# A new instruction clock for the planner, and weight halves merged, in a two-layer hybrid block on one Trainium2 core

## The chip, the cores and the metric

The kernel runs on one core of one Trainium2 chip. The metric is the device time of one execution in microseconds (us), read as the median of several runs. The engines are named as in the profile: PE is the tensor engine (PEld its weight loads), DVE the vector engine, ACT the scalar engine, POOL the GpSimd engine, SP the sync engine, whose queue issues nearly all DMAs.

## What is computed

The reference is two layers of a hybrid block over 256 tokens with 2048 features, all in 32-bit floats:

```python
for l in range(DEPTH):                                  # DEPTH = 2
    h = rms_norm(x, attn_norm_g[l])
    proj = h @ w_in[l]                                  # 2048 -> 3664
    y_ssd = ssd_mixer(proj[..., :c0], proj[..., c0:c1], proj[..., c1:c2], ...)
    y_mla = mla_mixer(proj[..., c2:c3], proj[..., c3:c4], proj[..., c4:], ...)
    mixed = jnp.concatenate([y_ssd, y_mla], axis=-1) @ w_out[l]
    x = x + mixed
    x = x + memory_cross_attention(rms_norm(x, ...), rms_norm(mem, ...), ...)
    x = x + swiglu(rms_norm(x, ffn_norm_g[l]), w_gate[l], w_up[l], w_down[l])   # hidden 5632
```

`ssd_mixer` is a causal convolution over four tokens with SiLU, a state-space scan over two chunks of 128 tokens, a gate and a normalization. `mla_mixer` is causal attention of eight heads from two latents of 512 features.

## The kernel before

**Products in three parts.** Every large product takes 32-bit weights and activations apart into a rounded part (`hi`, the tensors ending in `h`) and the rest (`lo`, ending in `l`), and adds three products: x-high times w-high, x-high times w-low, x-low times w-high. A *chunk* is 512 rows of a weight by 512 columns (368 or 384 in some products). Its four row blocks of 128, two token tiles and three parts make 24 products on PE (`mm_chunk`, line 509), each 128x128 by 512 columns.

**Weights.** `load_w` (line 488) loads a chunk by one DMA into `raw` (three buffers). Before the change the chunk is then handled in two halves of two row blocks each: `hi` is a rounding copy of half of `raw`, made by `copy` on ACT or DVE, whichever the planner finds free first (ACT in nearly all cases), and `lo` is `raw` minus `hi`, made on DVE. Each has six buffers of half a chunk. The very first chunk is loaded and handled in four pieces.

**Order.** No engine's order is that of the program text. A `Recorder` collects all instructions, and `issue()` (line 269) runs a rough clock over them: at each step it gives every engine the instruction of its own that can start first by the clock (ties by program order, with `hi` and `lo` of weights 400 places ahead of theirs), takes the earliest of all, and advances that engine's clock by `cost()` (line 243). Results are ready a fixed `LAG` of 0.35 us after the end; a transposing DMA counts 2.2 us on its queue and 1.6 us more until it has landed. The chosen order is then fixed: on the chip each engine and each queue runs its list in that order, and an instruction whose data isn't there holds up all that stand behind it on its engine.

**Stages of a layer.** First the latent projections, then three `conv_part`s (line 775; the third makes `bcT`, the B and C of the scan, which PE then transposes or multiplies), `ssd_prep` (line 942), two gate products `z_part`, four `ssd_core`s (line 1014), `ssd_finish` (line 1043), and four `mla_proj` / `mla_attn` pairs (lines 819 and 885). `out_proj` (line 1094) begins with the scan's part of its input (`ysT`) and goes on with the attention's part (`ymT`). Cross-attention and the feed-forward part follow. In `ssd_prep`, POOL makes `xd`, `xw` and `y` by seven instructions over 512 or 1024 elements a partition, next to the time at which DVE makes `bcT` by twelve multiply-adds.

Of the kernel before, what the change touches and what calls it, by code (L numbers as in the profile page):

```python
# [8 lines left out]
F32 = mybir.dt.float32  # L9
# [7 lines left out]
P = 128  # L17
# [22 lines left out]
# the vectors of a layer that have a value per feature: column and number of blocks of 128 features  # L40
# [12 lines left out]
class View:  # L53
    """a view of a tile that is allocated only when its first instruction is issued."""
# [84 lines left out]
class Slot:  # L139
    """a tile of a pool; slots of a pool's tag are given out by the scheduler."""  # L140
# [47 lines left out]
class Recorder:  # L188
    """Instructions in program order; issue() gives them to Tile in an order in which, by a rough
    clock, each engine always takes the first of its instructions that has its data."""  # L190
# [13 lines left out]
    def add(self, *ways):  # L204
        """one instruction; `ways` are the (engine, method, function, arguments) that it may be issued as."""
# [37 lines left out]
    def cost(self, engine, method, args, kw, writes, reads):  # L243
# [7 lines left out]
        if engine == "PE":  # L251
            n = args[0].free_size()
            if method == "transpose":
                return 0.1075, self.LAG
            passes = 1 if args[1].tile.dtype == F32R else 4
            return max(passes * n / 2400 + 0.003, 0.107), self.LAG
        ptr = sum(0.07 for v in reads if v.free_size() == 1)
        if engine == "ACT":
            return 0.09 + n * 0.833e-3 + ptr, self.LAG
# [7 lines left out]
        return 0.065 + n * (0.52e-3 if fast else 1.04e-3) + ptr, self.LAG  # L267

    def issue(self, margin):
# [18 lines left out]
        def slot_time(op):  # L288
            """when the slots that op's new tiles need are free; None when they are not to be given yet"""
# [18 lines left out]
        while left:  # L308
# [30 lines left out]
            at[e] = start + cost  # L339
            op.end = at[e] + lag  # L340
# [31 lines left out]
def hybrid_kernel(ctx: ExitStack, tc: tile.TileContext, const, vec, rows, x_in, x_tr, mem, mem_tr, positions, w_in, w_q_b,  # L372
# [6 lines left out]
    def copy(out, src, scale=None, engines=(A, V)):  # L379
        """out = src * scale, on whichever of the engines is free first."""  # L380
# [30 lines left out]
    def nm(s):  # L411
        uid[0] += 1
        return f"{s}_{uid[0]}"
# [4 lines left out]
    def chunk_T(name):  # L418
        """a chunk of 512 features, transposed: the part of 12 significant bits and the rest."""
        return b4([P, 4, S], name + "h", F32R), b4([P, 4, S], name + "l", F32R)  # L420
# [21 lines left out]
    # zero-padded rotary queries of the two heads of a pair  # L442
# [6 lines left out]
    # until the first weights are there, products that nothing reads start the tensor engine's full clock  # L449
# [26 lines left out]
    def rsqrt(v, shape, tag):  # L476
        """1/sqrt(v) for positive v."""
# [10 lines left out]
    def load_w(w, r0, c0, n, pieces=1):  # L488
        """512 rows and n columns of w: the parts of 12 significant bits and the rests, two row blocks a tile."""
        parts = []  # L490
# [6 lines left out]
        for half in range(2):  # L497
            hi = wpool.tile([P, 2, n], F32R, tag="hi", name=nm("hi"), bufs=6)
            lo = wpool.tile([P, 2, n], F32R, tag="lo", name=nm("lo"), bufs=6)
            for i in range(0, 2, 4 // max(pieces, 2)):  # L500
                k = slice(i, i + 4 // max(pieces, 2))
                rk = raw[:, 2 * half + k.start:2 * half + k.stop, :]
                copy(hi[:, k, :], rk)
                V.tensor_sub(lo[:, k, :], rk, hi[:, k, :].bitcast(F32))
            parts.append((hi, lo))
        rec.bias += 400
        return parts

    def mm_chunk(accs, xc, parts, n, first, last, tokens_outer=False):
        """accs[t] += x chunk (512 features, transposed, two parts) @ w chunk."""  # L510
        order = [(k, t) for k in range(4) for t in range(NT)]
        for k, t in sorted(order, key=lambda kt: kt[1]) if tokens_outer else order:
            hi, lo = parts[k // 2]
# [792 lines left out]
```

## Time and profile before

| | before |
|---|---|
| median of 3 runs | 2313.14 us (2311.99 to 2314.82) |
| span of the profiled execution | 2308.3 us |
| PE busy | 2288.8 us (99%) |
| DVE busy | 1458.9 us (63%) |
| ACT busy | 1242.4 us (54%) |
| POOL busy | 106.0 us (5%) |
| DMA, mean rate over the span | 203 GB/s |

The span runs from the first to the last instruction; the measured time lies 4.8 us above it. A product's record overlaps the next one, since the engine is pipelined; the distance from one start to the next tells what a product costs, and that is how PE's rows are read below. A wait is shown in brackets: the idle time before the instruction and what ended it.

### The profile page before, as it was taken

How to read it: one execution, taken by the hardware profiler on the slowest of the kernel's cores; microseconds unless marked ns; L12 is line 12 of the kernel's file. 1: busy time of each engine (PE TensorE's matmuls, PEld its weight loads, DVE VectorE, ACT ScalarE, POOL GpSimd, SP SyncE). 2: the span in 40 equal slices, each digit the busy share in tenths (PEclk: the TensorE clock that was granted, in tenths of full speed). 3: DMA queues.
4: the chain of work that ended last, by engine and by line, in shares of the span. 5: the costliest groups of instructions: out<-in, count | busy, mean ns of one | idle time of the engine just before them, and what ended most of it. 6: DMA issues, size and time to landing. Idle time of an engine off the chain costs nothing.

```text
span 2308.3 us, 27311 instructions
## 1 busy us (share of the span) xinstructions
PE 2288.8 (99%) x10454; PEld 1911.4 (83%) x10454; DVE 1458.9 (63%) x2068; ACT 1242.4 (54%) x1839; POOL 106.0 (5%) x92
## 2 busy tenths in 40 slices
PE   9999999999999999999999999999999999999999
PEld 8878888888888888888898688888888888888887
DVE  7888876755545555455768887767555455554554
ACT  7767666644434444344566586666444344444442
POOL 0030200000000000000000311000000000000000
PEclk9999999999999999999999999999999999999999
DMA  9856687666656666566777566766676566665664
GB/s 311 244 161 182 183 259 215 183 198 209 210 188 200 208 201 208 186 208 199 212 221 223 150 186 191 227 199 185 199 212 208 186 208 200 201 210 184 207 208 139
DMA packets 361269, 467.91 MB, mean 203 GB/s; under 512 B 142385, under 2 KB 165553, under 8 KB 361137
## 3 DMA queue, kind: packets, MB, share of 16 engines
q1 hardware_dynamic: 361104, 466.16, 65.9%
q8 instruction: 82, 1.34, 0.3%
q14 instruction: 51, 0.41, 0.1%
q0 software_dynamic: 32, 0.00, 0.0%
HBM read 429.94 MB, written 2.10 MB: 187 GB/s over the span
## 4 chain that ended last, share of the span: by engine, by line
PE 93%; DVE 4%; DMA 1%; ACT 1%; issue 1%; SPq 0%; POOL 0%; ACTq 0%
PE acc L368 89%; PE tp L368 4%; DVE lo L368 2%; DMA ht<-hs 1%; DVE bcT L368 1%; ACT hi L368 0%; DMA raw<-in_w_in_dram 0%; DVE ysTl L368 0%; DVE whole L368 0%; DVE hs L368 0%; DVE kv L368 0%; DVE dec L368 0%; SPq L368 0%; POOL qkr L368 0%; ACT xTh L368 0%
## 5 line engine op out<-in xcount | busy, mean ns | idle before, releaser
L368 DVE TENSOR_TENSOR lo<-raw,hi 128x1024 fp32r<-128x1024 f32 (+3 forms) x818 | 984.8, 1205 | 764.4 <-ACT hi L368 762.2
L368 ACT CAST hi<-raw 128x1024 fp32r<-128x1024 f32 (+3 forms) x817 | 842.1, 1032 | 933.6 <-PE acc L368 870.9
L368 PE MATMUL acc<-hi,xTh 128*128 128x512 f32 (+1 forms) x1984 | 762.5, 384 | 1.3 <-ACT hi L368 1.3
L368 PE MATMUL acc<-lo,xTh 128*128 128x512 f32 (+1 forms) x1984 | 762.5, 384 | 1.1 <-DVE lo L368 0.9
L368 PE MATMUL acc<-hi,xTl 128*128 128x512 f32 (+1 forms) x1984 | 763.0, 385 | 0.0
L368 PEld LDWEIGHTS acc<-hi,xTh 128*128 128x128 f32 x1984 | 372.9, 188 | 72.8 <-ACT hi L368 2.6
L368 PEld LDWEIGHTS acc<-lo,xTh 128*128 128x128 f32 x1984 | 373.2, 188 | 72.2 <-DVE lo L368 1.9
L368 PEld LDWEIGHTS acc<-hi,xTl 128*128 128x128 f32 x1984 | 373.2, 188 | 71.0 <-issue 1.3
L368 PE MATMUL acc<-hi,hTh 128*128 128x512 f32 x704 | 273.5, 389 | 0.0
L368 PE MATMUL acc<-lo,hTh 128*128 128x512 f32 x704 | 273.5, 389 | 0.0
L368 PE MATMUL acc<-hi,hTl 128*128 128x512 f32 x704 | 273.5, 389 | 0.0
L368 PEld LDWEIGHTS acc<-lo,hTh 128*128 128x128 f32 x704 | 132.2, 188 | 27.5
L368 PEld LDWEIGHTS acc<-hi,hTl 128*128 128x128 f32 x704 | 132.1, 188 | 27.4
L368 PEld LDWEIGHTS acc<-hi,hTh 128*128 128x128 f32 x704 | 132.2, 188 | 27.4
L368 DVE TENSOR_TENSOR x<-x,acc 128x512 f32<-128x512 f32 x80 | 51.5, 681 | 13.3 <-PE acc L368 13.3
L368 POOL TENSOR_TENSOR rx_y<-rx_v,mhalf 128x2 f32<-128x2 f32 x6 | 8.1, 1352 | 1039.5 <-DVE rx_v L368 1004.7
L368 PE MATMUL acc<-lo,ysTh 128*128 128x512 f32 x128 | 51.4, 401 | 0.0
L368 PE MATMUL acc<-hi,ysTh 128*128 128x512 f32 x128 | 51.1, 399 | 0.0
L368 PE MATMUL acc<-hi,mTh 128*128 128x512 f32 x128 | 51.1, 399 | 0.0
L368 PE MATMUL acc<-lo,mTh 128*128 128x512 f32 x128 | 50.5, 395 | 0.0
L368 PE MATMUL acc<-hi,ysTl 128*128 128x512 f32 x128 | 50.5, 395 | 0.0
L368 PE MATMUL acc<-lo,ymTh 128*128 128x512 f32 x128 | 50.2, 393 | 0.0
(274 smaller groups left out, 1999.5 us busy)
## 6 DMA issues: line engine op xcount, KB each, us to landing
raw<-in_w_gate_dram SPq DMA_DIRECT2D x88, 1024.0 KB, 5.2
raw<-in_w_up_dram SPq DMA_DIRECT2D x88, 1024.0 KB, 5.3
raw<-in_w_down_dram SPq DMA_DIRECT2D x88, 1024.0 KB, 5.0
raw<-in_w_in_dram SPq DMA_DIRECT2D x40, 1024.0 KB, 5.5
raw<-in_w_out_dram SPq DMA_DIRECT2D x32, 1024.0 KB, 5.6
raw<-in_w_in_dram SPq DMA_DIRECT2D x23, 736.0 KB, 5.2
raw<-in_w_kv_b_dram SPq DMA_DIRECT2D x8, 1024.0 KB, 5.1
raw<-in_w_xk_dram SPq DMA_DIRECT2D x8, 1024.0 KB, 5.4
```

The source lines that it names most:

```text
L368: fn(*args, **kw)
```

## The change

Three things are edited: the price list `cost()`, one rule in `issue()`, and the granularity of `load_w` (with `mm_chunk`, which reads it).

- Prices in `cost()`: a rounded product of n columns goes from n / 2400 + 0.003 us to (n + 32) / 2400 us, a transpose on PE from 0.1075 to 0.067 us, a 32-bit product from four passes to two passes of twice the columns; the fixed part of an instruction on ACT goes from 0.09 to 0.2 us, with 0.19 us more for one that also writes a sum, and on DVE from 0.065 to 0.135 us. `LAG`, the DMA prices and POOL's prices stay.
- Rule in `issue()`: once a POOL instruction of more than 0.5 us (powers excepted) is given out, DVE's clock is moved to that instruction's end, if it isn't there yet.
- `load_w`: one `hi` and one `lo` instruction for a whole chunk of four row blocks. Buffers go from six halves to three wholes, the same bytes. The first chunk stays in four pieces.

Comments and docstrings are removed as well; nothing else of the kernel's text is touched. The core of the diff:

```diff
@@ cost
         if engine == "PE":
             n = args[0].free_size()
-            if method == "transpose":
-                return 0.1075, self.LAG
-            passes = 1 if args[1].tile.dtype == F32R else 4
-            return max(passes * n / 2400 + 0.003, 0.107), self.LAG
-        ptr = sum(0.07 for v in reads if v.free_size() == 1)
+            if method == "transpose" or args[1].tile.dtype == F32R:
+                return max(n + 32, 160) / 2400, self.LAG
+            return 2 * max((2 * n + 32) / 2400, 0.1), self.LAG
+        ptr = sum(0.06 for v in reads if v.free_size() == 1)
         if engine == "ACT":
-            return 0.09 + n * 0.833e-3 + ptr, self.LAG
+            return 0.2 + n * 0.833e-3 + ptr + (0.19 if "accum_out" in kw else 0.0), self.LAG
...
-        return 0.065 + n * (0.52e-3 if fast else 1.04e-3) + ptr, self.LAG
+        return 0.135 + n * (0.52e-3 if fast else 1.04e-3) + ptr, self.LAG
@@ issue
             at[e] = start + cost
+            if e == "Pool" and cost > 0.5 and op.ways[e][5].get("op") != ALU.pow and "DVE" in at:
+
+                at["DVE"] = max(at["DVE"], at[e])
@@ load_w
-        for half in range(2):
-            hi = wpool.tile([P, 2, n], F32R, tag="hi", name=nm("hi"), bufs=6)
-            lo = wpool.tile([P, 2, n], F32R, tag="lo", name=nm("lo"), bufs=6)
-            for i in range(0, 2, 4 // max(pieces, 2)):
-                k = slice(i, i + 4 // max(pieces, 2))
-                rk = raw[:, 2 * half + k.start:2 * half + k.stop, :]
-                copy(hi[:, k, :], rk)
-                V.tensor_sub(lo[:, k, :], rk, hi[:, k, :].bitcast(F32))
-            parts.append((hi, lo))
+        hi = wpool.tile([P, 4, n], F32R, tag="hi", name=nm("hi"), bufs=3)
+        lo = wpool.tile([P, 4, n], F32R, tag="lo", name=nm("lo"), bufs=3)
+        for i in range(pieces):
+            k = slice(4 // pieces * i, 4 // pieces * (i + 1))
+            copy(hi[:, k, :], raw[:, k, :])
+            V.tensor_sub(lo[:, k, :], raw[:, k, :], hi[:, k, :].bitcast(F32))
         rec.bias += 400
-        return parts
+        return hi, lo
@@ mm_chunk
-            hi, lo = parts[k // 2]
-            wh, wl = hi[:, k % 2, :], lo[:, k % 2, :]
+            wh, wl = parts[0][:, k, :], parts[1][:, k, :]
```

## Rows read from the trace of the kernel before

**Rows 1.** The page: span, then busy time of each engine.

```profile
span 2308.3 us, 27311 instructions
PE 2288.8 (99%) x10454; PEld 1911.4 (83%) x10454; DVE 1458.9 (63%) x2068; ACT 1242.4 (54%) x1839; POOL 106.0 (5%) x92
```

**Rows 2.** Timeline of PE, undisturbed stretch: start us, length us, instruction.

```profile
1600.18 0.39 PE L368 MATMUL acc<-lo,xTh 128*128 128x512 f32 x1
1600.41 0.39 PE L368 MATMUL acc<-hi,xTl 128*128 128x512 f32 x1
```

**Rows 3.** Timeline of PE around the scan's first product, layer 0.

```profile
147.26 0.39 PE L368 MATMUL acc<-lo,xTh 128*128 128x512 f32 x1
152.42 0.56 PE L368 MATMUL tp<-cst,bcT 128*128 128x128 f32 x2 [4.78 <-ACT bcT L368]
152.63 0.78 PE L368 MATMUL acc<-hi,xTl 128*128 128x512 f32 x1
...
156.12 0.39 PE L368 MATMUL acc<-lo,xTh 128*128 128x512 f32 x1
```

**Rows 4.** Timeline of PE at the same place, layer 1.

```profile
1291.26 0.39 PE L368 MATMUL acc<-hi,xTh 128*128 128x512 f32 x1
1296.05 0.69 PE L368 MATMUL tp<-cst,bcT 128*128 128x128 f32 x2 [4.41 <-ACT bcT L368]
1296.39 0.78 PE L368 MATMUL acc<-lo,xTh 128*128 128x512 f32 x1
...
1298.24 0.63 PE L368 MATMUL acc<-hi,xTl 128*128 128x512 f32 x1
```

**Rows 5.** Stretches: us, busy (x count) of PE, PEld, DVE, ACT, POOL, clock, DMA.

```profile
135.00:148.00 13.00, 12.64 (x56) 10.14 (x54) 12.56 (x9) 7.68 (x10) 12.52 (x7) 1.00 0.56 170
148.00:160.00 12.00, 7.58 (x27) 5.19 (x27) 10.27 (x17) 6.30 (x9) 2.91 (x2) 0.86 0.51 153
160.00:173.00 13.00, 13.00 (x63) 10.19 (x62) 6.25 (x8) 8.53 (x13) 6.62 (x3) 1.00 0.18 62
173.00:205.00 32.00, 32.00 (x176) 27.88 (x175) 24.02 (x40) 20.97 (x45) 1.11 (x2) 1.00 0.41 129
519.00:577.00 58.00, 58.00 (x257) 48.06 (x256) 32.22 (x33) 26.62 (x29) 0.00 (x0) 1.00 0.69 210
```

**Rows 6.** Groups by form: line, engine, operation, shapes, count | busy us, mean ns.

```profile
L368 DVE TENSOR_TENSOR lo<-raw,hi 128x1024 fp32r<-128x1024 f32 x752 | 925.9, 1232 | 736.7 <-ACT hi L368 735.0
L368 ACT CAST hi<-raw 128x1024 fp32r<-128x1024 f32 x752 | 791.3, 1053 | 889.0 <-PE acc L368 836.0 <-issue 17.1 <-ACT hTh L368 15.5
...
L368 DVE TENSOR_TENSOR lo<-raw,hi 128x736 fp32r<-128x736 f32 x46 | 41.6, 924 | 21.6 <-ACT hi L368 21.3
L368 ACT CAST hi<-raw 128x736 fp32r<-128x736 f32 x45 | 35.4, 808 | 29.3 <-PE acc L368 21.3 <-DMA raw<-in_w_in_dram 7.2 <-DVE xTl L368 0.8
```

**Rows 7.** Timeline of DVE while POOL works, then after, layer 0.

```profile
137.95 5.76 DVE L368 TENSOR_TENSOR lo<-raw,hi 128x1024 fp32r<-128x1024 f32 x2
143.64 4.80 DVE L368 SCALAR_TENSOR_TENSOR bcT<-xbT,vecs,bcT 128x255 f32<-128x255 f32 x4
...
149.50 1.65 DVE L368 SCALAR_TENSOR_TENSOR bcT<-xbT,vecs,bcT 128x253 f32<-128x253 f32 x4
```

**Rows 8.** Timeline of POOL over the same stretch.

```profile
135.40 4.39 POOL L368 TENSOR_TENSOR xd<-xs,dt 128x1024 f32<-128x1024 f32 x2 [67.72 <-DVE lo L368]
139.75 2.88 POOL L368 TENSOR_TENSOR xw<-xd,w 128x1024 f32<-128x1024 f32 x1
142.60 5.57 POOL L368 TENSOR_TENSOR y<-xs,vecs 128x512 f32<-128x512 f32 x4
```

**Rows 9.** Timeline of the start: ACT, then PE's first product with `lo`.

```profile
11.70 0.81 ACT L368 CAST hi<-raw 128x736 fp32r<-128x736 f32 x1 [2.35 <-DMA raw<-in_w_in_dram]
14.09 0.43 PE L368 MATMUL acc<-lo,xTh 128*128 128x368 f32 x1 [0.93 <-DVE lo L368]
```

**Rows 10.** Timeline, layer 0: DVE's last rests of `ysT`, PE's first product with it.

```profile
226.31 1.68 DVE L368 SCALAR_TENSOR_TENSOR ysTl<-whole,vecs,ysTh 128x256 fp32r<-128x256 f32 x4
232.04 0.39 PE L368 MATMUL acc<-hi,ysTh 128*128 128x512 f32 x1
```

More of the change, by code (lines that the diff above doesn't have):

```diff
@@ L488, in load_w @@
     def load_w(w, r0, c0, n, pieces=1):
-        parts = []
         raw = wpool.tile([P, 4, n], F32, tag="raw", name=nm("raw"), bufs=3)
```

## The prediction

> **What bounds the kernel now.** I read the page's busy times first: PE is busy for 2288.8 of 2308.3 us [rows 1], so whatever the change does to DVE, ACT or the order, it can only win what PE loses by waiting or by running slowly. The second view is PE's timeline in an undisturbed stretch: one product of 512 columns starts 0.227 us after the one before [rows 2]. The change leaves the number and size of products as they are, so this part of the time can't move. The third view is PE's timeline where the page's busy share drops. There are two large places, the same one in each layer: the first transposes of `bcT`, for which PE waits on ACT [rows 3, 4]. Around them the stretches show two things more: the granted clock is 0.86 in the 12 us after the wait of layer 0, that is the lower of the two levels (1.2 instead of 2.4 GHz) for part of it, and DVE is full (12.56 of 13 us) while POOL is full as well (12.52 of 13) [rows 5]. In the feed-forward stretch PE is busy for 58.00 of 58 us with DVE at 32.22 and ACT at 26.62 [rows 5]: nothing to win there, and much room on the other engines.
>
> What order can win is thus at most PE's idle time, 2308.3 - 2288.8 = 19.5 us [rows 1], plus some 3.4 us of half clock (0.14 of 12 us in layer 0, taken twice) [rows 5]: 23 us, 1%. Some of it lies at the start and behind the last product and stays.
>
> **Part 1, the clock.** What does a stall of `bcT` cost? In layer 0 the product before it starts at 147.26, the transposes at 152.42: 5.16 us less one product's 0.23, 4.93 us. Then eight starts lie between 152.63 and 156.12, 3.49 us where 8 x 0.227 = 1.81 would do: 1.68 us of low clock. Sum 6.6 us [rows 2, 3]. In layer 1: 4.79 - 0.23 = 4.56 us, and four starts from 1296.39 to 1298.24 take 1.85 us instead of 0.91, 0.94 us: sum 5.5 us [rows 4]. Together 12.1 us. The scan's transposes stand too early in PE's list; behind them wait products whose weights are there (the next one starts 0.21 us after the transposes [rows 3]). If the new clock puts the transposes 5 us later, those products fill the gap.
>
> Does it? The old prices say 0.065 + 1024 x 1.04e-3 = 1.13 us for a `lo`, 0.943 for a `hi`; the rows say 1.232 and 1.053 [rows 6]. From 135 to 160 DVE runs 9 + 17 = 26 instructions [rows 5]; at 0.07 us too little each: 1.8 us. Larger is POOL: while it works, four multiply-adds of `bcT` take 4.80 us, 1.20 each, and outside that 1.65 us, 0.41 each; two `lo` take 5.76 us instead of 2.46 [rows 6, 7]. The old clock knows nothing of it and is 4 x 0.79 + 3.3 = 6.5 us too early; the new rule moves DVE behind each POOL instruction. Against that, PE's own price rises from 0.216 to 0.227, 5%, so that about 1.2 us less of other products fit into these 25 us. The clock's `bcT` moves back by about 1.8 + 6.5 - 1.2 = 7.1 us against a wait of 4.9: enough, with 2.2 us to spare.
>
> What eats the spare: the rule is one-sided. The rows show turns: four `y` of POOL last 5.57 us and four multiply-adds 4.80 in the same stretch [rows 7, 8], so POOL waits for DVE as DVE waits for POOL. The two `lo` spent (5.76 - 2.46) / 2 = 1.65 us each on POOL's part of a turn; a turn with one whole `lo` (2.33 us, part 2) is then 4.0 us, where the clock sees POOL's 0.15 + 1024 x 2.2e-3 = 2.4. Two such turns put `bcT` 3.2 us later than the clock thinks. The transposing DMAs keep their price too. So what is left of the wait lies between 0 and 3.2 us a layer; nearest are the rows of this stretch, which show two `lo` in it, but as halves, not wholes: I take 1 us a layer, 2 us in all. The Trainium skill ("SBUF — State Buffer", section "Who interferes with whom") has the ports that DVE and GpSimd share as an exclusive lock: a DVE instruction with two SBUF inputs and a GpSimd instruction that reads SBUF exclude each other, whoever comes second waits fully. The rows agree (1.20 us for 0.41 us of work, turn by turn). By that rule, held from both sides, the residual wait would stand at its upper end and the time at 2308.2 instead of 2303.8; by the change's one-sided hold it would be 2301.8.
>
> All other reordering moves DMAs as well (weights, transposes, all on SP's queue, which is listed by the same clock). In the feed-forward part the order has one answer, the list is steady, and I cost it at nothing: the cover is the stock of weights, next part.
>
> **Part 2, whole chunks.** Per chunk, ACT loses a fixed part: slope (1053 - 808) / 288 = 0.85 ns an element, so a whole `hi` takes 1.053 + 1024 x 0.85e-3 = 1.92 us for 2 x 1.053; a whole `lo`, by (1232 - 924) / 288 = 1.07, 2.33 us for 2 x 1.232 [rows 6]. That frees 376 x 0.18 = 68 us of ACT and 376 x 0.13 = 50 us of DVE, beside PE's work: worth 0 on the path. The price is the stock. `hi` waits for a buffer that PE frees (836 us of 889 of its idle time [rows 6]), so the makers are always as far ahead as buffers allow. Before: five halves of 12 products, 13.6 us, less 1.05 + 1.23, 11.3 us ahead. After: two wholes of 24 products, 10.9 us, less 1.92 + 2.33, 6.6 us ahead. A turn with POOL adds 1.65 us, four multiply-adds ahead of `lo` 4.8 us [rows 7]: 0.15 left. So I cost the merge at 0 in the body; if that cover went, PE would wait 1 to 2 us a layer, inside the bounds above.
>
> At the start there is no stock. The second chunk lands at 11.70; `hi` was made as two pieces of 736 side by side, PE's first product with `lo` started at 14.09 [rows 9]. A whole `hi` of 1472 takes 0.81 + 736 x 0.85e-3 = 1.43 us, `lo` 0.92 + 736 x 1.07e-3 = 1.71: 11.70 + 3.14 = 14.84, 0.75 us later, and the start of a kernel that PE bounds is paid in full. Bounds: 0.3 if DVE makes `hi`, 2 if later chunks slip too. I take 0.8.
>
> **Sum.** Against the profiled span: 2308.3 - 12.1 + 2.0 + 0.8 = 2299.0; the median lies 4.8 us above the span, so 2303.8 us.
>
> **The rivals.** *Given back at the scan's output.* PE now arrives 5.5 to 6.6 us earlier at its first product with `ysT`. Its data were ready at 226.31 + 1.68 = 228.0, the product started at 232.04: 4.05 us of slack [rows 10]. If DVE's chain up to there doesn't move, PE waits 2.5 us in layer 0 and 1.5 in layer 1: 2307.8, some 2 us more if the clock drops. For it: DVE is full where that chain is prepared. Against: DVE has 13 - 6.25 + 32 - 24.02 = 14.7 us idle from 160 to 205 [rows 5], and PE's products that feed it come earlier too.
>
> *Slower: the scan comes too late.* The new hold is also too strict: it gives DVE one instruction a POOL turn, with weights' `lo` in front. If three whole `lo` and none of the four multiply-adds run in POOL's stretch, the multiply-adds and the chain behind them move back by up to 4 x 0.41 + 2 x 2.33 = 6.3 us. PE then passes `bcT` without a wait and stands before `ysT`, for 2 + 6.3 = 8.3 us plus 1.7 of low clock, 10 us a layer: 2313.1 - 12.1 + 0.8 + 20 = 2321.8. It decides from a delay of 2 us on: there a wait of 4 plus the clock eats the 5.65 us that a layer has won. For it: nothing else is left for PE at that point (before 232 it has used up the attention's projections). Against: such a delay must first pass DVE's 14.7 us of idle time.
>
> *The order doesn't change where it matters.* Both waits stay, the start costs 0.8: 2313.9. For it: `LAG` and the DMA prices, which rule long chains, stay.
>
> **How the numbers follow.** Forecast 2303.8, chance 0.60. Given back 0.12, too late 0.18, no effect 0.07, better than 2294 0.03 (small waits gone as well, up to half of the rest of 23 - 12 us). The range reaches from 2294 (no residual, start 0.3, some small waits gone) to 2318, halfway into the slower rival; it leaves out some 0.15 above and 0.03 below. A measurement of this kernel can tell about 0.2%, 4.6 us. Faster by more: the forecast but for a rest (0.57), half of given back, the better case: 0.65. Slower by more: most of too late, 0.16. Within: 0.19.
>
> **What would show it.** Right: PE's wait before the products of `bcT` at most 1 to 2 us in both layers, clock 1.00 in the stretches behind it, half as many `hi` and `lo`, whole `hi` at 1.9 and `lo` at 2.3 us, PE's first `lo` product of the second chunk near 14.8 us, feed-forward stretches still at full PE. Wrong: a wait of several us before the first product of `ysT` or among the attention's products (rivals one and two), PE waiting for `lo` in POOL's stretch (the stock was too small), or the wait for `bcT` still there (the clock was still too early).

## The result, and the profile after

The kernel with the change takes 2335.59 us (2335.16 to 2336.11), the kernel before, on the same chip, 2312.56 us (2310.77 to 2314.82): ratio 1.0104, 95% interval 1.0092 to 1.0117. It is 23 us slower. The forecast was 2303.8 us with a range of 2294 to 2318: the sign was wrong and the range missed it.

First view of after, the page: span, then the busy time of each engine.

```profile
span 2334.3 us, 26186 instructions
PE 2300.8 (99%) x10454; PEld 1917.1 (82%) x10454; DVE 1433.9 (61%) x1737; ACT 1139.1 (49%) x1353; POOL 117.0 (5%) x95
```

Beside [rows 1], the span grew by 26.0 us. PE runs the same 10454 products, but is busy for 12.0 us longer (in part products at the lower clock, which last longer; see the last section) and idle for 33.5 us instead of 19.5, 14.0 us more. ACT has 103 us less work and DVE 25 less, and nothing of that reached the span: PE was the bound and is. The spans are those of one execution each, and the two differ by more than the medians do: wherever a run's span is listed, its time lies 1.7 to 1.9 us above it. Of the 4.8 us between span and median before, some 3 us are therefore that the profiled execution was one of the faster ones, and 26.0 us of span are 23 us of median.

Second view, the stretches of [rows 5] and some more: PE, PEld, DVE, ACT, POOL busy (x count), granted clock, DMA. After:

```profile
148.00:160.00 12.00, 11.99 (x53) 9.58 (x52) 10.35 (x5) 5.15 (x6) 11.92 (x7) 1.00 0.54 177
160.00:173.00 13.00, 10.28 (x29) 7.09 (x30) 9.07 (x10) 8.20 (x12) 9.93 (x5) 0.74 0.36 129
173.00:205.00 32.00, 28.77 (x155) 23.96 (x154) 22.95 (x39) 18.33 (x34) 0.00 (x0) 0.95 0.28 83
...
400.00:465.00 65.00, 60.96 (x279) 48.81 (x278) 47.81 (x79) 38.73 (x72) 3.30 (x3) 1.00 0.60 186
519.00:577.00 58.00, 58.00 (x257) 48.06 (x256) 30.14 (x20) 23.47 (x15) 0.00 (x0) 1.00 0.63 207
...
1385.00:1443.00 58.00, 51.77 (x258) 43.00 (x256) 45.20 (x118) 40.05 (x109) 15.70 (x15) 0.91 0.63 167
1616.00:1674.00 58.00, 56.79 (x242) 46.57 (x243) 30.25 (x27) 24.44 (x21) 0.73 (x1) 0.97 0.57 179
```

Before, the three of these that [rows 5] do not have:

```profile
400.00:465.00 65.00, 65.00 (x305) 53.95 (x304) 47.90 (x82) 44.32 (x81) 1.63 (x1) 1.00 0.60 179
1385.00:1443.00 58.00, 57.44 (x296) 47.98 (x295) 45.27 (x113) 39.02 (x96) 11.15 (x12) 1.00 0.69 191
1616.00:1674.00 58.00, 58.00 (x257) 48.02 (x257) 30.96 (x31) 25.80 (x27) 0.00 (x0) 1.00 0.66 201
```

The hole of before, 148 to 160 with PE at 7.58 of 12 us, is full now (11.99). New holes stand where before had none, or next to none: 160 to 205 (PE was at 13.00 and 32.00 there [rows 5]), 400 to 465, and in layer 1 from 1385 and from 1616 on.

Third view, what PE waited for in after: us in total, times, longest.

```profile
PE tp L370 <- POOL qkr L370: 5.8, 3, 4.6
PE tp L370 <- POOL rb L370: 3.7, 2, 2.7
PE acc L370 <- DVE zs L370: 3.2, 1, 3.2
PE tp L370 <- DVE qkT L370: 2.3, 2, 1.5
PE acc L370 <- DVE xTl L370: 2.2, 2, 1.1
PE acc L370 <- ACT xTh L370: 2.1, 2, 1.0
PE acc L370 <- ACT ysTh L370: 1.5, 1, 1.5
```

The two waits for `bcT` [rows 3, 4] are gone. In their place stand more waits, most of them shorter (one of 4.6 us is as long), for other tiles, on three engines. Two of them in PE's timeline:

```profile
176.69 1.20 PE L370 MATMUL tp<-rb,lrow 64*128 64x512 f32 x4
181.12 0.44 PE L370 MATMUL acc<-hi,qaTh 128*128 128x384 f32 x1 [3.23 <-DVE zs L370]
182.01 0.69 PE L370 MATMUL tp<-cst,bcT 128*128 128x128 f32 x2
...
1390.62 0.39 PE L370 MATMUL acc<-hi,kvaTl 128*128 128x512 f32 x1
1395.58 1.30 PE L370 MATMUL tp<-cst,qkr 128*128 128x128 f32 x3 [4.57 <-POOL qkr L370]
```

`bcT` comes at 182.01 instead of 152.42 [rows 3]. Counting products into `acc` in PE's timeline, 771 stand ahead of it instead of 677; ahead of the first one with `ysT` there are 960 in both kernels. So 94 products of filler that the list had kept for the time behind `bcT` are spent before it.

Where the 26.0 us arise, from the starts of the same PE products in both traces (each column is what that section takes more than in before; the last two rows are experiments told below):

| kernel | start to last `xb` | to first `ysT` | to last `ymT` | to first `oT` | to first `hT` | to layer 1, last `xb` | to `ysT` | to `ymT` | to `oT` | to the end | sum |
|---|---|---|---|---|---|---|---|---|---|---|---|
| after | 1.6 | 5.1 | 2.6 | 0.3 | 5.6 | 0.5 | 2.4 | 1.2 | 0.0 | 6.7 | 26.0 |
| e_act_price | 2.2 | 0.0 | 0.8 | 5.8 | 0.0 | 0.2 | -2.3 | 7.1 | 6.4 | 0.5 | 20.7 |
| e_dve_halves | 0.1 | -3.9 | 1.8 | 0.8 | 0.1 | 0.1 | 0.7 | 0.2 | 0.1 | -0.6 | -0.6 |

In after, the scan's sections (to `ysT`) lose 5.1 and 2.4 us although the two waits for `bcT` are gone from them, and the section from the first `oT` to the first `hT` takes 5.6 us more (in layer 1 this lies inside the 6.7). Not all of this is loss: in after, 16 products (eight with `xpr`, eight with `xvn`) stand behind the first `oT` that before has ahead of it. By the starts in other rows (four `xpr` in 0.44 us, two `xvn` in 0.44) they are worth some 2.6 us, an estimate. So about 3 us are lost in the cross-attention, whose 0.3 looks too good by as much, and about 3 us behind it, on the way to the feed-forward, a place that the prediction does not mention. Its rows, ACT first, then PE:

```profile
448.90 1.92 ACT L370 CAST hi<-raw 128x2048 fp32r<-128x2048 f32 x1 [2.62 <-PE acc L370]
450.72 0.63 ACT L370 ACTIVATE junk<-x 128x512 f32<-128x512 f32 x1
...
453.85 0.51 ACT L370 ACTIVATE xTh<-whole,vecs 128x256 fp32r<-128x256 f32 x1
455.95 1.91 ACT L370 CAST hi<-raw 128x2048 fp32r<-128x2048 f32 x1 [1.58 <-PE acc L370]
457.76 0.91 ACT L370 ACTIVATE xTh<-whole,vecs 128x256 fp32r<-128x256 f32 x2
```

```profile
456.66 0.61 PE L370 MATMUL acc<-hi,xTl 128*128 128x512 f32 x2
458.31 0.50 PE L370 MATMUL acc<-hi,xTh 128*128 128x512 f32 x1 [1.04 <-ACT xTh L370]
...
459.12 0.40 PE L370 MATMUL acc<-lo,xTh 128*128 128x512 f32 x1
460.63 0.73 PE L370 MATMUL acc<-hi,xTl 128*128 128x512 f32 x2 [1.12 <-DVE xTl L370]
```

This is a queue blocked at its head. ACT stands at a `hi` for 1.58 us because its buffer is still read by PE, then works 1.8 us on it; the `xTh` at 457.76, listed behind it, starts the moment ACT is free, and PE, at 458.31, has waited for that `xTh`.

### The profile page after: what moved, and what is told of

It reads as the page before. It is cut to its first block, busy times and chain, and to the rows that moved or that the text cites. A ratio compares the mean times of both kernels' runs of the same rounds, so it can differ in the third digit from the quotient of the medians.

```text
span 2334.3 us, 26186 instructions
## 1 busy us (share of the span) xinstructions
PE 2300.8 (99%) x10454; PEld 1917.1 (82%) x10454; DVE 1433.9 (61%) x1737; ACT 1139.1 (49%) x1353; POOL 117.0 (5%) x95
## 4 chain that ended last, share of the span: by engine, by line
PE 90%; DVE 4%; DMA 3%; ACT 1%; issue 1%; POOL 1%; SPq 0%; POOLq 0%; ACTq 0%; DVEq 0%
PE acc L370 86%; PE tp L370 4%; DMA ht<-hs 2%; DVE lo L370 2%; ACT hi L370 1%; DVE bcT L370 0%; SPq L370 0%; DMA raw<-in_w_in_dram 0%; POOL y L370 0%; DVE xTl L370 0%; DVE hs L370 0%; DVE whole L370 0%; POOL pr L370 0%; ACT xpr L370 0%; DVE x L370 0%
## 5 line engine op out<-in xcount | busy, mean ns | idle before, releaser
L370 DVE TENSOR_TENSOR lo<-raw,hi 128x2048 fp32r<-128x2048 f32 (+3 forms) x411 | 922.5, 2245 | 695.3 <-ACT hi L370 694.6
L370 ACT CAST hi<-raw 128x2048 fp32r<-128x2048 f32 (+3 forms) x411 | 765.9, 1864 | 958.3 <-PE acc L370 890.0
L370 DVE COPY h<-ht 128x1024 uint16<-128x1024 uint16 x44 | 30.7, 754 | 50.6 <-DMA ht<-hs 50.6
L370 ACT ACTIVATE h<-acc,rx_y 128x512 f32<-128x512 f32 x44 | 30.0, 686 | 56.3 <-PE acc L370 56.3
L370 PE MATMUL acc<-hi,ymTh 128*128 128x512 f32 x128 | 50.1, 394 | 0.1
```

What stands on the lines that cost most here:

```text
L370: fn(*args, **kw)
```

## The experiments

All of them compute everything. In the table "A", "D", "P", "H" are the new prices of ACT, DVE and PE and the hold behind a POOL instruction; the scalar's price (`ptr`, 0.06 or 0.07) goes with A or D unless the diff says otherwise. Each ratio is to the kernel before on the same chip.

| kernel | weights | clock | us | ratio [95%] |
|---|---|---|---|---|
| e_dve_halves | halves | P H D | 2309.44 | 0.9993 [0.9984, 1.0003] |
| e_pe_hold_halves | halves | P H | 2311.37 | 0.9998 [0.9989, 1.0007] |
| e_b_lag36, e_b_lag33, e_jitter | halves | old, `LAG` 0.36, 0.33, 0.34 | 2314.84, 2317.82, 2320.4 | 1.0012, 1.0028, 1.0031 |
| e_true_clock35 | halves | P H, 0.19 for sums | 2324.7 | 1.0055 [1.004, 1.007] |
| e_clock_only | halves | P H D A | 2330.5 | 1.0087 [1.007, 1.0104] |
| e_true_clock | halves | P H, 0.09 for sums, `LAG` 0.12 | 2350.75 | 1.0164 [1.0149, 1.0179] |
| e_dve_price | whole | P H D | 2315.26 | 1.0014 [1.0004, 1.0024] |
| e_old_act_dve | whole | P H | 2319.0 | 1.0040 [1.0025, 1.0055] |
| e_merge_only | whole | old | 2319.97 | 1.0038 [1.0025, 1.0051] |
| e_no_sums | whole | P H D, A without sums | 2326.97 | 1.0068 [1.0051, 1.0084] |
| e_act_price | whole | P H A | 2330.78 | 1.0079 [1.0064, 1.0094] |
| e_whole_tiles | whole buffers, half instructions | old | 2330.67 | 1.0080 [1.0064, 1.0097] |
| e_a_lag36, e_lag01, e_a_lag34 | whole | all new, `LAG` 0.36, 0.1, 0.34 | 2331.09, 2332.49, 2332.9 | 1.0082, 1.0083, 1.0090 |
| e_no_hold | whole | P D A | 2333.01 | 1.0098 [1.0083, 1.0113] |
| after | whole | P H D A | 2335.59 | 1.0104 [1.0092, 1.0117] |

**The two parts apart: e_merge_only, e_clock_only.** The kernel before with the merge of `load_w` and `mm_chunk` alone, and the kernel after with the halves of before.

```diff
-        for half in range(2):
-            hi = wpool.tile([P, 2, n], F32R, tag="hi", name=nm("hi"), bufs=6)
+        hi = wpool.tile([P, 4, n], F32R, tag="hi", name=nm("hi"), bufs=3)
...
```

> Before, with only the merge of the weight halves; clock and hold as before. Theory A (the higher prices of ACT and DVE make the planner place the long chains late and use up PE's independent products early): no loss from the merge, 2308 to 2316 us, and the 4.4 to 4.8 us waits before the first transposes of bcT remain. Theory B (the hold of DVE behind POOL): the same, 2308 to 2316. Theory C (whole chunks are too coarse; the stock of 6.6 us isn't enough): about 2335. Theory D (any other order than that of before loses, whatever made it): 2320 to 2340.

> The new clock (all prices and the hold) with weight halves as before. Theory A: 2330 to 2340 us, as after. Theory B: 2330 to 2340. Theory C: 2300 to 2316, the forecast's gain without the loss. Theory D: 2320 to 2340.

Measured: 2319.97 and 2330.5 us. Both parts lose, and the clock loses more: 0.38% and 0.87%. The merge alone changes the list too, and there the `bcT` waits stay (10.0 us in total). So neither part keeps what the prediction gave it.

**The hold, and both engines' prices: e_no_hold, e_old_act_dve.** After without the hold, and after with ACT's and DVE's old prices.

```diff
-            if e == "Pool" and cost > 0.5 and op.ways[e][5].get("op") != ALU.pow and "DVE" in at:
-                at["DVE"] = max(at["DVE"], at[e])
```

```diff
-            return 0.2 + n * 0.833e-3 + ptr + (0.19 if "accum_out" in kw else 0.0), self.LAG
+            return 0.09 + n * 0.833e-3 + ptr, self.LAG
...
-        return 0.135 + n * (0.52e-3 if fast else 1.04e-3) + ptr, self.LAG
+        return 0.065 + n * (0.52e-3 if fast else 1.04e-3) + ptr, self.LAG
```

> After, without the rule that moves DVE behind a POOL instruction. Theory A: most of the loss stays, 2325 to 2340 us, and the bcT wait comes back in part. Theory B: the loss goes, 2305 to 2316. Theory C: 2330 to 2340. Theory D: 2320 to 2340.

> After, with the old fixed prices of ACT and DVE (0.09 and 0.065 us, no surcharge for sums, 0.07 a scalar operand); PE's new prices, the hold and the whole chunks stay. Theory A: the loss goes, 2300 to 2316 us, and PE's waits in the attention's and cross-attention's products shrink. Theory B: 2330 to 2340. Theory C: 2330 to 2340. Theory D: 2320 to 2340.

Measured: 2333.01 and 2319.0 us. The hold, which the prediction's second rival made the culprit, is worth nothing in sum that can be told here. It does change what PE waits for. PE's waits for `bcT` in e_no_hold, then in e_b_lag33 (told further below): us in total, times, longest.

```profile
PE tp L367 <- ACT bcT L367: 9.8, 2, 5.4
```

```profile
PE tp L368 <- ACT bcT L368: 0.6, 2, 0.3
```

Without the hold both waits for `bcT` are back, as long as in before; with it they are gone, and the waits for `qkr`, `rb` and `zs` stand in after instead (12.7 us in the view above; none of the three is in the list of e_no_hold). And e_b_lag33, the kernel before with a `LAG` of 0.33 us, has next to no wait for `bcT` and is slower than before. So to pass `bcT` without a wait is not by itself a gain. With the old prices the time is that of the merge alone (ratios 1.0040 and 1.0038): all that the clock costs comes with ACT's or DVE's price.

**Buffer or instruction: e_whole_tiles.** The whole buffers of the merge, but each `hi` and `lo` made by two instructions over 256 rows.

```diff
-        for i in range(pieces):
-            k = slice(4 // pieces * i, 4 // pieces * (i + 1))
+        parts = max(pieces, 2)
+        for i in range(parts):
+            k = slice(4 // parts * i, 4 // parts * (i + 1))
```

> The merge alone lost 0.38%. Here the buffers are wholes as in that run (three of four row blocks), but each is still filled by two hi and two lo instructions of half a chunk; clock and hold as before. Theory E (the wait of a hi for a whole buffer that PE frees only every 5.4 us holds up what stands behind it on ACT): the loss stays, 2316 to 2323 us beside a before of 2310.6. Theory F (it is the length of the instruction, 1.9 and 2.3 us that nothing can pass): the loss goes, 2308 to 2314. Theory D (any other order loses): 2314 to 2330.

Measured: 2330.67 us, slower than the merge and outside every range that was expected. It does not tell the two apart cleanly, because the list changed in a way that was not asked for: DVE is busy for 1622.1 us and ACT for 965.7, as the planner gave part of `hi` to DVE. So all that it says is that this list, with shorter instructions over whole buffers, is no better than the merge.

**How much any other list costs: e_jitter, e_b_lag33, e_b_lag36, e_a_lag34, e_a_lag36.** A change of `LAG` by 0.01 or 0.02 us has no meaning of its own, but it moves 318 to 922 of PE's 10233 listed instructions. In before or in after:

```diff
-    LAG = 0.35
+    LAG = 0.34
```

> Before, with LAG 0.34 us instead of 0.35 and nothing else: 426 of 10233 places in PE's list change, no price of an engine does. Theory D (the order of before is a lucky one and any change of it costs some 10 us or more): 2318 to 2335 us. Theory A (the loss comes from ACT's and DVE's higher prices, so the planner is steady against small changes): 2306 to 2314.

> Before with LAG 0.33 us (778 of 10233 places in PE's list change). Theory D1 (the order of before is the best of many, any neighbour of it loses): 2314 to 2326 us beside a before of 2311 to 2313. Theory D2 (neighbours scatter to both sides, LAG 0.34 was an unlucky one): 2304 to 2322, not above in both of these runs.

> Before with LAG 0.36 us (318 of 10233 places in PE's list change). D1: 2314 to 2326 us. D2: 2304 to 2322.

> After with LAG 0.34 us (922 of 10233 places in PE's list change). Theory A (the new clock as such, through its longer prices on ACT and DVE, plans some 10 us or more worse than the old one): 2328 to 2342 us, above every neighbour of before. Theory D (the new clock only draws another order from the same lot): 2310 to 2345, overlapping with the neighbours of before.

> After with LAG 0.36 us (375 of 10233 places in PE's list change). Theory A: 2328 to 2342 us. Theory D: 2310 to 2345.

Measured: the neighbours of before lose 0.12, 0.28 and 0.31%, 2.8 to 7.2 us. The neighbours of after lose 0.82 and 0.90% to before, little less than after itself. So a list by itself is worth some 3 to 7 us, and before's is the best of its neighbourhood (two other lists, below, equal it); but the two neighbourhoods, four lists and three, stand 12 us apart at their nearest and some 17 us on average, and that is the change's. Each kernel of the table is one such list, so a step of less than some 7 us between two of them is shown only where several pairs agree.

**A clock that is right, and short latency: e_lag01, e_true_clock, e_true_clock35.** On DVE and ACT the record of an instruction overlaps the next one (last section), so the new prices, which are near the lengths of records, charge too much. e_true_clock has halves, PE's price and the hold, and start-to-start prices; e_lag01 is after with a `LAG` of 0.1. The core of e_true_clock's edit beside after (the halves come back as in before):

```diff
-    LAG = 0.35
+    LAG = 0.12
...
-            return 0.2 + n * 0.833e-3 + ptr + (0.19 if "accum_out" in kw else 0.0), self.LAG
+            return 0.09 + n * 0.833e-3 + ptr + (0.09 if "accum_out" in kw else 0.0), self.LAG
...
-        return 0.135 + n * (0.52e-3 if fast else 1.04e-3) + ptr, self.LAG
+        return 0.065 + n * (0.52e-3 if fast else 1.04e-3) + ptr, self.LAG
```

> After, with LAG 0.1 instead of 0.35 us. The new prices of ACT and DVE are lengths of records; the traces show the next instruction starting 0.08 us (DVE) and 0.10 us (ACT) before a record ends, so price plus LAG counts the latency twice. Theory G (what hurts is the latency of a chain as the clock sees it, price and LAG together): most of the loss goes, 2312 to 2322 us. Theory H (what hurts is the time that an engine is held, so that it seems fuller than it is): the loss stays, 2328 to 2338. Theory D: 2320 to 2340, anywhere.

> Weight halves as before; PE's new prices and the hold; ACT and DVE by the distance from start to start that the trace of before shows (fixed parts 0.09 and 0.065 us as before, 0.09 us more for a sum), and LAG 0.12 us. Theories A, G and H: a clock that counts neither twice gives no loss, 2298 to 2314 us, and bcT's wait below 2 us in both layers. Theory D: 2314 to 2335.

> The kernel of the run with start-to-start prices (halves, PE's new price, hold, ACT 0.09 us with 0.09 us for a sum, DVE 0.065 us), but with LAG 0.35 in place of 0.12. Theory L (the LAG of 0.35 us is slack that keeps a list from being cut too fine; the short LAG made that run slow): 2314 to 2324. Rival M (the prices made it slow): 2340 to 2352.

Measured: 2332.49, 2350.75 and 2324.7 us. The first is what theory H expected: the loss stays. The second is far outside all that was expected: the most truthful prices gave the slowest kernel of all. With `LAG` back at 0.35 most of that is gone, some 25 us by the ratios; the step is not quite pure, since e_true_clock35 charges 0.19 us for a sum, not 0.09. Beside e_pe_hold_halves it differs by that charge and 0.01 us a scalar alone, and loses 13.3 us by it. That a `LAG` longer than the latency works as slack fits this pair, but not e_lag01: there the short `LAG` cost nothing (ratio 1.0083, after 1.0104). Before with the short one was not tried, so why e_true_clock is so slow stays open.

**Which engine's price: e_act_price, e_dve_price, e_pe_hold_halves.** After with DVE's old price; after with ACT's old price; before with PE's price and the hold alone. The lines are those of the diff above, one at a time.

> The kernel after with DVE's old price (0.065 us + slope); ACT's new price (0.2 us + slope, 0.19 us for a sum), PE's price, the hold and whole chunks stay. Known: all new prices 2335, both engines' old prices 2319. Theory I (the weights' rounding stands first on ACT; it is ACT's price that makes the clock put chain steps behind it): most of the 16 us comes back, 2328 to 2335. Theory J (DVE's price, since DVE is full around the scan): 2316 to 2323. Theory K (only both together do harm): within 4 us of 2319. The planner's own clock sees 22.6 us of idle PE in this list, against 8.5 us in the list of the next kernel and 39.7 us in the one of after; if that view counts, this one is the slower of the two.

> The kernel after with ACT's old price (0.09 us + slope); DVE's new price (0.135 us + slope), PE's price, the hold and whole chunks stay. Theory I (ACT's price does the harm): 2316 to 2323. Theory J (DVE's): 2328 to 2335. Theory K (only both): within 4 us of 2319. The planner's own clock sees 8.5 us of idle PE here.

> The kernel before with PE's new price and the hold behind a POOL instruction, nothing else: halves, ACT's and DVE's old prices. Theory A (the systematic part comes from ACT's and DVE's prices): no more than what the neighbours of the kernel before lose, 2314 to 2321. Rival (a new PE price by itself makes the list worse, since every due time hangs on PE): 2325 to 2331, as the run with all new prices over halves. If the clock's purpose is met by PE's price and the hold alone, the waits for bcT are gone and the time lies below the kernel before, 2300 to 2308.

Measured: 2330.78, 2315.26 and 2311.37 us. This is theory I: ACT's price does the harm. Taking it out of after gives back 0.90 points of the ratio (1.0104 to 1.0014), 21 us. Where DVE's price is the old one, it costs less: 0.39 points, 9 us (e_old_act_dve, 1.0040, to e_act_price, 1.0079). PE's price and the hold change nothing (0.9998).

One place shows how. With DVE's price and without ACT's (e_dve_price), ACT and then PE in the cross-attention of layer 0:

```profile
399.55 0.56 ACT L370 ACTIVATE xpr<-tp,nb,fq_y 128x256 f32<-128x256 f32 x1 [3.42 <-PE tp L370]
...
401.73 1.90 ACT L370 CAST hi<-raw 128x2048 fp32r<-128x2048 f32 x1
403.53 0.59 ACT L370 COPY xpT<-tp 128x512 f32<-128x512 f32 x1
...
407.03 0.69 ACT L370 ACTIVATE xvn<-acc,rstd_m 128x512 f32<-128x512 f32 x1 [0.22 <-PE acc L370]
407.71 1.90 ACT L370 CAST hi<-raw 128x2048 fp32r<-128x2048 f32 x1
```

```profile
407.95 0.60 PE L370 MATMUL tp<-xpT,xvn 128*128 128x256 f32 x2
```

With ACT's price and without DVE's (e_act_price), the same, ACT and then PE:

```profile
407.88 0.56 ACT L370 ACTIVATE xpr<-tp,nb,fq_y 128x256 f32<-128x256 f32 x1 [2.96 <-DVE nb L370]
408.35 0.19 ACT L370 ACTIVATION_READ_ACCUMULATOR xpr<-tp,nb,fq_y 128x1 f32 x1
408.44 0.56 ACT L370 ACTIVATE xpr<-tp,nb,fq_y 128x256 f32<-128x256 f32 x1
408.89 0.19 ACT L370 ACTIVATION_READ_ACCUMULATOR xpr<-tp,nb,fq_y 128x1 f32 x1
408.99 1.90 ACT L370 CAST hi<-raw 128x2048 fp32r<-128x2048 f32 x1
410.78 0.56 ACT L370 ACTIVATE xpr<-tp,nb,fq_y 128x256 f32<-128x256 f32 x1
...
414.90 1.90 ACT L370 CAST hi<-raw 128x2048 fp32r<-128x2048 f32 x1 [0.75 <-PE acc L370]
416.71 0.56 ACT L370 ACTIVATE xpr<-tp,nb,fq_y 128x256 f32<-128x256 f32 x1
...
418.28 1.27 ACT L370 ACTIVATE xvn<-acc,rstd_m 128x512 f32<-128x512 f32 x2
```

```profile
414.70 1.04 PE L370 MATMUL tp<-cst,xpr 128*128 128x128 f32 x8
419.02 1.13 PE L370 MATMUL tp<-xpT,xvn 128*128 128x256 f32 x4 [3.29 <-ACT xvn L370]
```

With DVE's price alone, eight `xpr` have one `hi` among them: four, `hi`, four, then `xvn`, 69.9 us after PE's last product with `ymT`. With ACT's price they have two: two, `hi`, four, a `hi` that waits for PE, two, then `xvn`, 75.9 us after that product. PE waits 3.29 us for it, once in each layer, and the section loses 5.8 and 6.4 us. The second `hi` is half of the 6.0 us: the first `xpr` already starts 65.5 us after that product instead of 62.5, and from there to `xvn` it is 10.4 us instead of 7.5. What made the first 3 us was not followed up. An `xpr` takes 0.47 + 0.09 = 0.56 us from start to start; the new price says 0.2 + 256 x 0.833e-3 + 2 x 0.06 + 0.19 = 0.72. So on the new clock the next `hi` falls due after fewer such steps; that link is argued from the prices, what stands in which order is in the rows. After itself, which has both prices, does not lose in this form: its section up to the first `oT` has other products in it and loses about 3 us (above).

The price also sways who copies: the `hs` copies, 284 in each kernel, are 80 on ACT in before, 48 with DVE's price alone, 15 with ACT's price alone and 21 in after; the others stand on DVE. Whether that costs anything by itself was not tried.

**Which half of it, and the best of what is left: e_no_sums, e_dve_halves.** After without the charge for sums; halves with PE's price, the hold and DVE's price.

```diff
-            return 0.2 + n * 0.833e-3 + ptr + (0.19 if "accum_out" in kw else 0.0), self.LAG
+            return 0.2 + n * 0.833e-3 + ptr, self.LAG
```

> The kernel after without the 0.19 us that ACT's price adds for an instruction with a sum; its 0.2 us base and all else stay. Theory N (the base, 0.11 us more on each of ACT's instructions, does the harm): 2329 to 2336, as after. Theory O (the sums do it: each norm and each score square then holds the clock's ACT for 0.28 us more than the trace's 0.09): 2313 to 2320, as after with ACT's old price. The planner's own clock sees 37.2 us of idle PE in this list, as in the one of after (39.7): by that view N is right.

> Halves, PE's new price, the hold, DVE's new price; ACT's old price. Theory P (without ACT's price the new clock is harmless, and what is left are the few us by which any other order differs): 2308 to 2319; the planner's clock sees 7.6 us of idle PE. Rival (a price on one of the two engines that share the copies tilts the choice between them and costs by itself): 2322 to 2331. To beat the kernel before, both waits for bcT would have to go and nothing to come: 2300 to 2305.

Measured: 2326.97 and 2309.44 us. Neither N nor O: the sums' charge is worth 0.36 points (1.0104 to 1.0068), the base 0.54 (1.0068 to 1.0014), 8 and 12 us, each one pair and not much above what any other list costs. (The 0.28 us in the text above is a slip: a charge of 0.19 beside the trace's 0.09 is 0.10 us too much.) In e_dve_halves one wait for `bcT` is left:

```profile
PE tp L370 <- ACT bcT L370: 4.1, 1, 4.1
```

Its table row above tells the rest: 3.9 us won in the scan of layer 0, then 1.8, 0.8 and 0.7 us given back in the sections behind. Its interval includes 1: nothing that ran is shown to beat the kernel before.

**The sum of it.** ACT's price costs time in each of the three pairs that differ by it: 21 us over whole chunks with DVE's new price (e_dve_price to after), 9 us with DVE's old one (e_old_act_dve to e_act_price), and 0.94 points, 22 us, over halves (e_dve_halves to e_clock_only). Whole chunks cost 0.17 to 0.42 points, 4 to 10 us, in four pairs that differ by nothing else; each of these is no more than another list can cost, and what speaks for the merge as the cause is that all four have the same sign. DVE's price has no fixed sign: -1 us over halves, -6 us over whole chunks without ACT's price (e_old_act_dve to e_dve_price), +6 us with it (e_act_price to after). So no single sum divides the 24 us (0.0104 x 2312). By one row of kernels from before to after, PE's price, the hold and DVE's price come to -2 us, whole chunks to 5, ACT's price to 21; by another (e_pe_hold_halves, e_old_act_dve, e_act_price, after), to -0.5 for PE's price and the hold, 9.7 for whole chunks, 9.0 for ACT's price, 5.8 for DVE's. Either sum comes out by construction, since its steps are the differences of a row of kernels. It is not one wait that costs the time either. Each list loses at other places (the table of sections). How ACT's price leads to a loss was shown at one place, the cross-attention of e_act_price, and there for half of it; the place around 456 costs nothing with ACT's price and without DVE's (0.0 in the table), so it takes more than ACT's price.

The planner's own clock, read from its list as it writes it, is a warning that was there to be read: it has PE idle, the start included, for 5.1 us in before, 4.7 in e_pe_hold_halves, 7.6 in e_dve_halves and 8.5 in e_dve_price, but for 22.6 in e_act_price, 37.2 in e_no_sums, 39.7 in after and 41.0 in e_clock_only. It takes the first instruction that has its data and does not search for a list that is short. But a small figure promises nothing: 6.2 in e_whole_tiles, 5.1 in e_true_clock.

## Why the prediction was wrong

**What bounds the kernel.** Right: PE. Nothing here speaks against the limit of 23 us for a gain either; what it lacked was a limit for a loss. The same views that say "PE waits for little" say that the old list is good in a hundred places, each of which a new list can spoil.

**Part 1, `bcT`.** That the hold takes the waits away was right: both are gone in after, the residual of 2 us is 0, and without the hold they are back (9.8 us in e_no_hold). Even this hangs on small things: in e_a_lag34, after with a `LAG` shorter by 0.01 us, one wait of 5.5 us is back in layer 1. The size of the move was wrong: 29.6 us later instead of 7.1, at the cost of 94 products of filler. Part of it is not the clock's: the merge alone, to which the prediction gave none, puts the transposes at 164.79 (e_merge_only), 12.4 us later. Wrong above all was the worth, 12.1 us for the end of the two waits: with and without the hold the time is the same (2335.59 and 2333.01 us), and the first product with `ysT` starts at 238.7 and 238.3 us. PE lacks work around this place all the same: in after it waits for `rb` and `zs` ahead of `bcT` in layer 0, and for `qkr` behind it in layer 1. Where a part is won at the scan, as in layer 0 of e_dve_halves (3.9 us) or layer 1 of e_act_price (2.3), other sections take it back.

**The step that failed** is the passage "All other reordering moves DMAs as well [...] In the feed-forward part the order has one answer, the list is steady, and I cost it at nothing". In the steady stretch that was right (PE 58.00 of 58 from 519 to 577). Everywhere else it was costed at nothing without being looked at: the attention's products, the cross-attention, the transposes ahead of the feed-forward. If the 12.1 us of part 1 are counted as won, as the prediction did, and 1.6 as lost at the start, 26.0 + 12.1 - 1.6 = 36.5 us have to be put against that zero and the zero of the merge (4 to 10 of them, part 2); what is spent around the scan to end the two waits is part of them. The neighbours show that even a meaningless change of `LAG` costs 3 to 7 us, so no reordering is costed at nothing.

**A second step failed beneath it**: "at 0.07 us too little each" for DVE. It takes the length of a record (1.232 us [rows 6]) for the time that the engine is held. [Rows 7] speak against it: four in 1.65 us are 0.41 each, as the prediction itself worked out, while the record of one such instruction lasts 0.47 (mean of the eight in before). The sum has one more slip: the 4.8 us from span to median are 1.8 us and a fast execution (above). ACT's price, on which most of the loss hangs, was not weighed at all: the prediction prices ACT's `hi` and goes on.

**Part 2.** The durations came as worked out (1.92 and 2.33 us; 1.43 and 1.71 at the start):

```profile
L370 DVE TENSOR_TENSOR lo<-raw,hi 128x2048 fp32r<-128x2048 f32 x376 | 866.5, 2305 | 659.1 <-ACT hi L370 658.6
L370 ACT CAST hi<-raw 128x2048 fp32r<-128x2048 f32 x376 | 719.2, 1913 | 926.2 <-PE acc L370 866.7 <-DVE x L370 56.3 <-issue 3.0
L370 DVE TENSOR_TENSOR lo<-raw,hi 128x1472 fp32r<-128x1472 f32 x23 | 38.9, 1691 | 23.7 <-ACT hi L370 23.7
L370 ACT CAST hi<-raw 128x1472 fp32r<-128x1472 f32 x23 | 32.8, 1428 | 27.7 <-PE acc L370 19.4 <-DMA raw<-in_w_in_dram 8.0
```

So did the start: PE's first product with the second chunk's `lo` at 14.83, forecast 14.84, and 1.6 us in the first section, twice the 0.8 but inside the bounds.

```profile
14.83 0.44 PE L370 MATMUL acc<-lo,xTh 128*128 128x368 f32 x1 [1.13 <-DVE lo L370]
```

What failed is "I cost the merge at 0 in the body". The stock of weights, which that cost was argued from, did hold: PE waited for `lo` 1.1 us in all, once, at the start. The price was elsewhere: by the four pairs it costs 4 to 10 us. The likely way, shown at the place around 456 and argued for the rest, is this. A `hi` waits for a buffer (866.7 us of ACT's idle time, as much as the 836 of before [rows 6]), and whatever is listed behind it on ACT waits along. With 323 such waits instead of 578 each is longer (the longest 5.4 us instead of 3.7), so a step of the chain that stands behind one is later by more. The prediction asked what PE would lack, not who stands behind the instruction that waits.

**The rivals.** "The scan comes too late" came nearest (2321.8, chance 0.18): the chain did move back and PE did stand among the attention's products, 4.57 us in layer 1. Its mechanism, the hold, is there as well: it trades the waits for `bcT` for other waits around them. But in sum it is worth nothing (e_no_hold), so it is not what made the kernel slower, and its place holds 7.5 of the 26 us. (Of the rival "given back", one reading is not quite right: the four rests of `ysT` at 226.31 [rows 10] are not DVE's last; four more start at 229.66 and take 1.68 us. Its slack holds for the first four.) "Given back" is what happened to the gain in e_dve_halves. The chance for slower, 0.16, was taken from one mechanism at one place; the cases where the order is worse at a place not looked at had no chance of their own.

## What to carry to other kernels

A list that a greedy planner wrote, and that was kept because it was fast, is itself a tuned constant: change a price in a way that means nothing (a latency by 0.01) and see what that costs before crediting or blaming a better clock, and let no prediction cost "all other reordering" at zero. A price by the length of records charges too much; on ACT, which makes the weights' `hi` and shares the copies, it cost 9 to 22 us here, so ask who stands behind such an engine's instructions in its queue. But no run shows that a truer price is a faster list: the truest of these prices, with a short `LAG`, gave the slowest kernel. Where instructions that wait for buffers are merged, the time freed on an engine that is no bound buys nothing, while each wait at the head of its queue can grow (here from at most 3.7 to at most 5.4 us).

## What the hardware showed

The record of an instruction on DVE or ACT is longer than the engine is held. The next record starts some 0.1 us before the end on ACT: in the rows of e_act_price above a `hi` of 1.90 us starts at 408.99 and the next instruction at 410.78, 1.79 us on, while an `xpr` of 0.56 and its sum of 0.19 take 0.47 and 0.09. On DVE it is 0.08 us, in after:

```profile
1384.41 2.29 DVE L370 TENSOR_TENSOR lo<-raw,hi 128x2048 fp32r<-128x2048 f32 x1 [0.35 <-ACT hi L370]
1386.62 0.88 DVE L370 TENSOR_SCALAR y<-y,ry_y 128x512 f32<-128x512 f32 x2
```

1386.62 - 1384.41 = 2.21 us, not 2.29. The old prices of whole `hi` and `lo` (0.09 + 2048 x 0.833e-3 = 1.80, 0.065 + 2048 x 1.04e-3 = 2.19) meet these distances; the new ones (1.91, 2.26) lie near the records. The Trainium skill ("Perfetto Trace Analysis", section "Optimizing Scalar/DVE Operations") says the same: the profiled length holds the fixed overhead about twice, some 60 ns each time on DVE and 93 on Scalar in SBUF, since the half that waits for the write to be acknowledged overlaps with the next instruction. The traces agree in kind, with 80 ns on DVE and 110 on ACT in these rows; it is the rule that spoke against a clock set to record lengths, and the prediction did not use it.

The other surprise is the clock's share. By the granted clock of the stretches above, the lower level takes 0.26 of 13, 0.05 of 32, 0.09 of 58 and 0.03 of 58 us in after, 11.9 us of work, against 3.4 us in before: 8.5 us more, some of it while PE is idle anyway, behind waits that are each 1 to 5 us long. The same two waits of 1.0 and 1.1 us, for `xTh` and `xTl`, stand in both layers, and the clock falls behind them in layer 1 (0.97 from 1616 to 1674) but not in layer 0 (1.00 from 400 to 465). So the 12.0 us by which PE is busy for longer are not all clock. The record of a product (0.39 us where starts are 0.23 apart) also covers the first 0.16 us of a wait that follows it, and PE waits 26 times in after, 11 times in before. How the 12.0 us divide was not taken apart.
